# A seven-product form for two projections of a hybrid trunk layer, with low parts made by accumulating DMA

## The chip, the cores and the metric

The kernel runs on one core of a Trainium2 chip. The metric is the time of one execution on the device, in microseconds (us). In the views, PE is TensorE, PEld its weight load, DVE VectorE, ACT ScalarE, POOL GpSimd and SP SyncE.

## The reference

One layer with D = 1024 and 1024 positions, in f32, batch 1. Cut to what matters:

```python
h = rms_norm(x, norm_g) * (1 + scale) + shift           # scale, shift, gate from c
(sq, sk, sv, sz, dq, dk_, dv_, dz, db, da,
 lq, lk, lv, lz, lr, mg) = split(h @ w_in)              # one input projection
y_sb  = stick_breaking_attention(q, k, v) * silu(sz)    # 4 heads x 128  -> 512 wide
y_gdn = rms_norm(gated_delta_rule(...), gdn_onorm) * silu(dz)   # 512 wide
y_gla = rms_norm(gla_chunked(...), gla_onorm) * silu(lz)        # 4 heads x 256 -> 1024 wide
g_sb, g_gdn, g_gla = split(sigmoid(mg + merge_b), 3)    # three gates, D wide each
merged = g_sb*(y_sb @ proj_sb) + g_gdn*(y_gdn @ proj_gdn) + g_gla*(y_gla @ proj_gla)
return x + gate * (merged @ w_out)
```

The GLA projection and the output projection are products of 1024 x 1024 by 1024 x 1024; proj_sb and proj_gdn have 512 rows.

## The kernel before

Everything is kept transposed: 128 channels on the partitions, 1024 positions (two halves of 512, HALF) along the free dimension. Each f32 operand is split into a high part (a cast to a shorter form) and a low part (source minus high part), and a product takes three passes: high x high, high x low, low x high. `split` is a cast on ScalarE and a subtraction on VectorE (lines 151 and 152), or with a scale lines 154 and 155. `load_w` brings a weight of 128 columns in halves of 512 rows (256 KB, tile "raw") and splits each. `mm` (L95) issues every matmul; `run_cm` makes one group: two halves, each 3 x kt matmuls of 128x512 (kt is 8, or 4 for 512 rows) into one PSUM bank of the pool "acc", which has two banks, and then `evac` reads the bank.

TensorE's order is written out by hand (`emit`, `dense`): the mixers' steps are tasks with due times, and dense groups of the input projection fill the time between them. The other engines' orders are made by a scheduler. 18 of the 24 gate groups run early as fillers (`early_gate`) and keep their result in DRAM (`g_dram`); the mixers' results y go to DRAM too (`y_dram`: 0 to 3 SB, 4 to 7 GDN, 8 to 15 GLA).

After the last attention block comes the final stage, `final_groups`: GLA's first 512 rows for 8 column blocks d ("part", ScalarE copies the bank), then gates and GLA's other rows ("rest"), GDN ("add"), SB ("last"), and 8 groups of the output projection (`out_group`), whose operands are the split of the merged rows. There are 1440 matmuls of 128x512 in it: 6 gate groups x 48, 384 for GLA, 192 for GDN, 192 for SB, 384 for the output. `load_y` brings y in 512 KB pieces and splits them. The norm weights gla_onorm and gdn_onorm are multiplied into the weights proj_gla and proj_gdn when these are split, 128 rows at a time.

Of the kernel before, what the change touches and what calls it, by code (L numbers as in the profile page):

```python
# [19 lines left out]
P = 128  # L20
D = 1024
# [8 lines left out]
EARLY = [(g, d) for g in (1, 0, 2) for d in range(2, KT)]  # L30
# [22 lines left out]
def kernel(ctx: ExitStack, tc: tile.TileContext, xT: bass.AP, c: bass.AP,  # L53
# [6 lines left out]
    wp = ctx.enter_context(tc.tile_pool(name="wp", bufs=3))  # L60
# [96 lines left out]

    def raw_tile():
        return wp.tile([P, 4, P], F32, tag="raw", name="raw")

    def load_half(hi, lo, src, k0, scales=None):
        raw = raw_tile()
        nc.sync.dma_start(out=raw, in_=src[k0 * P:(k0 + 4) * P, :].rearrange("(k p) n -> p k n", p=P))
        if scales is None:
            split(hi, lo, raw)
        else:
            for k in range(4):
                split(hi[:, k, :], lo[:, k, :], raw[:, k, :], scales[k])
# [18 lines left out]
    def run_cm(w, evac, rhs=None, kt=KT):  # L187
        r_hi, r_lo = rhs or (h_hi, h_lo)
        late = getattr(evac, "late", None)
        for hf in range(2):  # L190
# [11 lines left out]
            evac(hf, sl, ps)  # L202
            yield

    def run_tm(w, evac):
        whi, wlo = w
        late = getattr(evac, "late", None)
        for t2 in range(CH // 2):
            ps = bank(pa, "acc", HALF)
            for j in range(2):  # L210
                ts = slice((2 * t2 + j) * P, (2 * t2 + j + 1) * P)
                n = 0
                for k in range(KT):
                    for r, b in ((h_hi, whi), (h_hi, wlo), (h_lo, whi)):
                        mm(ps[:, j * 256:(j + 1) * 256], r[k][:, ts], b[:, k, :], 109,
# [9 lines left out]
    # a dense group: (load, run); loads are issued one group ahead  # L225
# [103 lines left out]
    # the first head's four column groups advance together as h arrives  # L329
# [4 lines left out]
    for k in range(KT):  # L334
# [5 lines left out]
        w = wp.tile([P, 2, 4, P], F32R, tag="w", name="w")  # L340
# [387 lines left out]
    def gdn_scan(st, q):  # L728
# [49 lines left out]
        nc.vector.tensor_mul(out=y, in0=ps.rearrange("p c t -> p (c t)"), in1=st["z"][:, sl])  # L778
# [190 lines left out]
    def gla_scan(st, q):  # L969
# [37 lines left out]
        for o, t0, since in outs:  # L1007
# [8 lines left out]
            for e_ in range(2):  # L1016
                y = mid("w6", 256)
                nc.vector.tensor_mul(out=y, in0=ps[:, e_].rearrange("p i t -> p (i t)"),
                                     in1=st["z"][e_][:, t0:t0 + 256])
                nc.sync.dma_start(out=y_dram[8 + 2 * h + e_][:, t0:t0 + 256], in_=y)  # L1020

# [133 lines left out]
    merged = []  # L1155
    gate_t = {}
    ys = {}

    def gate_group(gi, d):
        def evac():  # L1160
            gate_t[gi, d] = mid("v0"), mid("v1")

            def f(hf, sl, ps):
                nc.scalar.activation(out=gate_t[gi, d][hf], in_=ps, func=AF.Sigmoid,
                                     bias=C("merge_b", gi * 8 + d))
            return f
        return cm_in(O_MG + gi * D + d * P, evac)

    def early_gate(gi, d):
# [13 lines left out]
        return cm_in(O_MG + gi * D + d * P, evac)  # L1183

    def fetch_gate(gi, d):
        def run(_):
            gate_t[gi, d] = mid("v0"), mid("v1")
            for hf in range(2):
                nc.sync.dma_start(out=gate_t[gi, d][hf],
                                  in_=g_dram[gi, d][:, hf * HALF:(hf + 1) * HALF])  # L1190
            return
            yield
        return (lambda: None), run

    def load_y(yi):
        hi, lo = [], []
        for k in range(4):
            yr = big("u3")
            nc.sync.dma_start(out=yr, in_=y_dram[yi + k])
            a, b = big(f"u{4 + k}", 1024, F32R), big(f"u{4 + k}", 1024, F32R)  # L1200
            split(a, b, yr)
            hi.append(a)
            lo.append(b)
        return hi, lo

    def proj_group(gi, proj, row0, yi, d, scales, mode):
        def evac(hf, sl, ps):
            if mode == "part":
                if hf == 0:
                    merged.append(big(("u0", "u1", "u2", "u8")[d // 2]))  # L1210
                nc.scalar.copy(out=merged[d][:, sl], in_=ps)
                return
# [171 lines left out]
```

## Time and profile before

| what | value |
|---|---|
| median of 3 runs | 1523.69 us (1520.3 to 1524.83) |
| span of the profiled execution | 1522.0 us |
| TensorE busy | 1463.0 us, 96% |
| VectorE busy | 861.8 us, 57% |
| ScalarE busy | 676.8 us, 44% |
| GpSimd busy | 175.8 us, 12% |
| TensorE in the final stage, 1181.5 to 1518.1 us | 336.56 of 336.60 us |
| mean granted clock | 0.987 |

The profiled execution's time is its span, 1522.0 us; no other time of it is given. Busy shares are over the whole span. The granted clock is a share of full speed.

### The profile page before, as it was taken

To read this page: it belongs to the slowest core of one execution; us is meant where nothing else is said; L and a number is where in the kernel's file an instruction comes from. 1 tells how busy PE (TensorE), PEld (TensorE's weight loads), DVE (VectorE), ACT (ScalarE), POOL (GpSimd) and SP (SyncE) were. 2 spreads that over 40 slices of the span, in tenths; PEclk is the share of its full clock that TensorE was granted. 3 is DMA by queue.
4 is the path that set the end of the run, shared out by engine and by line. 5 is a ranking of instruction groups with operands and counts; after the bars stand their busy time and mean duration, and the time that the engine had idled before them with its cause. 6 is when DMAs were issued, how large, how long until landed. Compare 5 with 4: busy or idle time off the path is not lost.

```text
span 1522.0 us, 26560 instructions
## 1 busy us (share of the span) xinstructions
PE 1463.0 (96%) x10564; PEld 1227.5 (81%) x10564; DVE 861.8 (57%) x1855; ACT 676.8 (44%) x1473; POOL 175.8 (12%) x306
## 2 busy tenths in 40 slices
PE   4898999999999999999999999999999999999998
PEld 1677787777778887978888999889988888888887
DVE  5978736557653666667666525563555226474621
ACT  4255845462652846556475524342444442322200
POOL 4231222223330000000000100000000000000000
PEclk8899999999999999999999999999999999999999
DMA  6644322131231211212121212111122334353342
GB/s 211 189 119 120 99 87 74 44 88 47 79 93 50 56 43 53 53 32 60 50 67 38 69 49 63 49 36 42 43 69 85 110 104 138 115 149 111 120 143 76
DMA packets 162470, 126.48 MB, mean 83 GB/s; under 512 B 23429, under 2 KB 139269, under 8 KB 162346
## 3 DMA queue, kind: packets, MB, share of 16 engines
q1 hardware_dynamic: 162202, 124.47, 27.9%
q8 instruction: 83, 1.36, 0.4%
q14 instruction: 41, 0.34, 0.1%
q10 hardware_dynamic: 144, 0.31, 0.1%
HBM read 99.80 MB, written 24.95 MB: 82 GB/s over the span
## 4 chain that ended last, share of the span: by engine, by line
PE 81%; DVE 9%; ACT 4%; POOL 2%; issue 2%; DMA 2%; SPq 0%; POOLq 0%; DVEq 0%; ACTq 0%
PE acc L95 66%; PE lv L95 6%; PE mx L95 6%; PE tr L122 3%; DVE u L299 1%; DVE w L152 1%; POOL c L284 1%; DVE u L386 1%; POOL u L453 1%; DVE w L570 1%; DVE w L572 1%; DVE u L1110 1%; DMA u<-in_adaT 1%; POOL w L596 0%; DMA w<-xd 0%
## 5 line engine op out<-in xcount | busy, mean ns | idle before, releaser
L95 PE MATMUL acc<-h_hi,w 128*128 128x512 f32 x1856 | 658.1, 409 | 12.4 <-ACT h_hi L151 5.7
L95 PEld LDWEIGHTS acc<-h_hi,w 128*128 128x128 f32 x1856 | 352.5, 190 | 84.5 <-ACT h_hi L151 6.1
L95 PE MATMUL acc<-h_lo,w 128*128 128x512 f32 x928 | 365.9, 394 | 8.1 <-DVE h_lo L358 7.7
L95 PEld LDWEIGHTS acc<-h_lo,w 128*128 128x128 f32 x928 | 176.9, 191 | 36.9 <-DVE h_lo L358 8.9
L95 PE MATMUL acc<-whi,h_hi 128*128 128x256 f32 x640 | 186.8, 292 | 0.0
L95 PE MATMUL acc<-whi,h_lo 128*128 128x256 f32 x640 | 180.7, 282 | 0.0
L95 PE MATMUL acc<-wlo,h_hi 128*128 128x256 f32 x640 | 180.7, 282 | 0.0
L95 PE MATMUL acc<-u,w 128*128 128x512 f32 x768 | 176.5, 391 | 0.0
L95 PEld LDWEIGHTS acc<-u,w 128*128 128x128 f32 x768 | 144.2, 188 | 31.6
L151 ACT CAST w<-raw 128x512 fp32r<-128x512 f32 x143 | 84.2, 619 | 121.8 <-PE acc L95 90.4
L152 DVE TENSOR_TENSOR w<-raw,w 128x512 fp32r<-128x512 f32 x143 | 98.5, 701 | 50.7 <-ACT w L151 49.9
L95 PEld LDWEIGHTS acc<-whi,h_hi 128*128 128x128 f32 x640 | 122.3, 191 | 1.4 <-issue 0.7
L95 PEld LDWEIGHTS acc<-wlo,h_hi 128*128 128x128 f32 x640 | 122.4, 191 | 0.1
L95 PEld LDWEIGHTS acc<-whi,h_lo 128*128 128x128 f32 x640 | 122.1, 191 | 0.0
L284 POOL TENSOR_TENSOR c<-c,mhalf 128x4 f32<-128x4 f32 (+1 forms) x56 | 54.7, 976 | 578.8 <-DVE c L282 577.4
L95 PE MATMUL acc<-m_hi,w 128*128 128x512 f32 x256 | 79.0, 389 | 0.0
L1110 DVE TENSOR_TENSOR_SCAN u<-u,zero_c 128x128 f32<-128x128 f32 (+7 forms) x32 | 43.4, 1356 | 36.1 <-ACT u L1108 36.1
L155 DVE SCALAR_TENSOR_TENSOR w<-raw,col,w 128x128 fp32r<-128x128 f32 x96 | 29.5, 349 | 55.3 <-ACT w L154 55.3
L95 PEld LDWEIGHTS mx<-r,u 128*128 128x128 f32 x288 | 44.1, 190 | 18.0 <-DVE r L751 4.9
L95 PEld LDWEIGHTS acc<-m_hi,w 128*128 128x128 f32 x256 | 48.0, 188 | 10.0
L95 PE MATMUL mx<-r,u 128*128 128x128 f32 x288 | 48.5, 281 | 6.3 <-POOL u L720 2.7
L95 PE MATMUL lv<-u,u 128*32 128x32 f32 (+5 forms) x528 | 49.2, 252 | 4.1 <-DVE u L653 4.1
(254 smaller groups left out, 2177.6 us busy)
## 6 DMA issues: line engine op xcount, KB each, us to landing
raw<-in_w_in SPq DMA_DIRECT2D x160, 256.0 KB, 3.0
u<-in_adaT SPq DMA_DIRECT2D x24, 512.0 KB, 3.5
g_dram<-v SPq DMA_DIRECT2D x36, 256.0 KB, 2.1
v<-g_dram SPq DMA_DIRECT2D x36, 256.0 KB, 2.6
u<-in_xT SPq DMA_DIRECT2D x16, 512.0 KB, 5.6
u<-y_dram SPq DMA_DIRECT2D x16, 512.0 KB, 3.8
v<-gam_d SPq DMA_DIRECT2D x16, 256.0 KB, 3.5
y_dram<-v SPq DMA_DIRECT2D x16, 256.0 KB, 2.0
```

Source lines behind the costliest of these rows:

```text
L95: return nc.tensor.matmul(out, lhsT=lhsT, rhs=rhs, **kw)
L122: nc.tensor.transpose(out=out, in_=in_, identity=ident[:k, :k])
L151: nc.scalar.copy(out=hi, in_=raw)
L152: nc.vector.tensor_sub(out=lo, in0=raw, in1=hi.bitcast(F32))
L155: nc.vector.scalar_tensor_tensor(out=lo, in0=raw, scalar=scale, in1=hi.bitcast(F32), op0=ALU.mult, op1=ALU.subtract)
L284: nc.gpsimd.tensor_tensor(out=out, in0=out, in1=mhalf[:, 0:n], op=ALU.pow)
L299: nc.vector.tensor_tensor_reduce(out=junk, in0=aw, in1=c_row, scale=1.0, scalar=0.0, op0=ALU.mult, op1=ALU.add, accum_out=mod[:, j:j + 1])
L386: nc.vector.scalar_tensor_tensor(out=t, in0=r[:, tap:tap + T], scalar=C("conv", j + tap), in1=t, op0=ALU.mult, op1=ALU.add)
L453: nc.gpsimd.tensor_scalar(out=gt[0][DA, sl], in0=raw[DA, :], scalar1=C("dt_bias")[DA, :], scalar2=None, op0=ALU.add)
L570: nc.vector.tensor_tensor(out=t3, in0=L3[:, w:16, j:w].broadcast_to([32, n, w]), in1=Xl3[:, j:w, 0:w].broadcast_to([32, n, w]), op=ALU.mult)
L572: nc.vector.tensor_sub(out=Xl3[:, w:16, 0:w], in0=Xl3[:, w:16, 0:w], in1=t3)
L1110: nc.vector.tensor_tensor_scan(om[:, 0:n][:, ::-1], om[:, 0:n][:, ::-1], zero_c.broadcast_to([P, n]), 1.0, ALU.mult, ALU.add)
```

## The change

**Seven products in place of eight.** The GLA and the output projection are taken as 2 x 2 blocks of 512: output columns d and d + 4 (d = p), the two halves of the positions, and the two halves of the 1024 rows. `strassen` makes a pair (p, p + 4) of output blocks from seven products of a combination of weight blocks (`PRODUCTS`) with a combination of operand blocks (`UNITS`: b11, t1, t2, b22, t3, b21, t4; t1 to t4 are differences). Each is 12 matmuls (4 row blocks x 3 passes), 84 for a pair, four pairs for a projection. Two PSUM banks accumulate: X takes units 0, 2, 4, 6 and W units 1, 3, 5; `read(i)` reads the bank after each unit.

**Operands of GLA.** The differences of y are formed during attention (tasks T.y0 to T.y3, `differences`: 4 loads, 4 subtractions and 4 stores each) and kept in DRAM; in the final stage each of 28 operands is loaded (256 KB), cast on ScalarE and subtracted on VectorE (`load_unit`).

**Operands of the output.** `out_operands(p)` is called after SB's group d = p + 4; its seven pieces form differences of the merged blocks and split them by `split_dma`: ScalarE writes the high part, then its negative into the low part, and GpSimd issues a DMA that adds the source to it. The weights of GDN, SB and the output use it as well, 72 in all.

**The rest.** All gates go through g_dram; six gate groups still run at the start of the final stage. The onorm weights are multiplied into y when it is made. The pool "raw" has 8 buffers where it had 3, the weight tiles are halved (6 for 3), the small weights are split in two halves, the order of the early gates is another, and the program has 4096 bytes for GpSimd's DMA descriptors. SB's and GDN's columns come in the order 0, 4, 1, 5, 2, 6, 3, 7.

```diff
+    def split_dma(hi, lo, raw):
+        nc.scalar.copy(out=hi, in_=raw)
+        nc.scalar.activation(out=lo, in_=hi.bitcast(F32), func=AF.Copy, scale=-1.0)
+        nc.gpsimd.dma_start(out=lo, in_=raw, accum_op=ALU.add)
...
+    def strassen(src1, src2, rhs, prepare, read, by_dma=False):
...
+        def run(loaded):
+            a, ws, context = loaded
+            ahead.pop(0)
+            while len(ws) < 3:
+                ws.append(part(a, len(ws)))
+            X, W = bank(pa, "acc", HALF), bank(pa, "acc", HALF)
+            for i, unit in enumerate(UNITS):
+                if i + 3 < 7:
+                    ws.append(part(a, i + 3))
+                else:
+                    early_part()
+                ps = X if i in (0, 2, 4, 6) else W
+                first, last = i in (0, 1, 5), i in (3, 5, 6)
+                n = 0
+                for p in range(4):
+                    for v, r in ((0, 0), (0, 1), (1, 0)):
+                        mm(ps, ws[i][:, v, p, :], rhs[p][unit][r], 216,
+                           start=(first and n == 0), stop=(last and n == 11),
+                           skip_group_check=True)
+                        n += 1
+                    if p == 1:
+                        yield
+                read(i, ps, context)
+                yield
...
+    def load_unit(tag, src):
+        hi, lo = new_unit(tag)
+        raw = lo.bitcast(F32)
+        nc.sync.dma_start(out=raw, in_=src)
+        nc.scalar.copy(out=hi, in_=raw)
+        nc.vector.tensor_sub(out=lo, in0=raw, in1=hi.bitcast(F32))
+        return hi, lo
...
+    def differences(n, p, get):
+        def sub(out, a, b, t):
+            nc.vector.tensor_sub(out=out, in0=a, in1=b)
+            nc.sync.dma_start(out=t_dram[n, p][t], in_=out)
...
+        def read(i, ps, xr):
...
+                nc.vector.scalar_tensor_tensor(out=x[:, ts], in0=ps[:, ts],
+                                               scalar=mod[:, 16 + d:17 + d], in1=x[:, ts],
+                                               op0=ALU.mult, op1=ALU.add)
...
     def final_groups():
...
+        gs = [gate(*e) for e in EARLY[sum(FILL):]]
+        gs[0] = after(lambda: gla_operands(FIRST_UNITS), gs[0])
+        gs += [after(lambda: gla_operands(("t3", "b21", "t4")), gla_pair(0))]
+        gs += [gla_pair(p) for p in range(1, 4)]
+        order = [d for p in range(4) for d in (p, p + 4)]
+        gs += [proj_group(1, proj_gdn, 4, d) for d in order]
+        gs += [proj_group(0, proj_sb, 0, d) for d in order]
+        gs += [out_pair(p) for p in range(4)]
+        return [(g, ["S.m3"]) for g in gs]
...
+    for p in range(4):
+        tasks.append((f"T.y{p}", lambda p=p: y_differences(p), ["L.s3.1", f"D.S{min(p, 2)}"], 0))
```

**First place: TensorE where one GLA column block or pair ends and the next begins.** In the kernel before, TensorE's list in the GLA part of the final stage reads so (acc_N is one use of a bank; u4 to u7 are y's parts, w a weight):

```order
L95 MATMUL acc_12864<-u6_12814,w_12789 128x512
L95 MATMUL acc_12864<-u6_12815,w_12789 128x512
L95 MATMUL acc_12864<-u6_12814,w_12789 128x512
L95 MATMUL acc_12864<-u7_12820,w_12789 128x512
L95 MATMUL acc_12864<-u7_12821,w_12789 128x512
L95 MATMUL acc_12864<-u7_12820,w_12789 128x512
L95 MATMUL acc_12879<-u4_12802,w_12789 128x512 [waits Activation_49]
L95 MATMUL acc_12879<-u4_12803,w_12789 128x512
L95 MATMUL acc_12879<-u4_12802,w_12789 128x512
```

Each new acc takes the other of the two banks. After the change, from the end of pair 0 to the start of pair 1 (acc_13491 is X of pair 0, acc_13492 its W; acc_13635 and acc_13636 are X and W of pair 1):

```order
L95 MATMUL acc_13492<-unit_13471,w_13539 128x512 x3
L95 MATMUL acc_13491<-unit_13475,w_13556 128x512 [waits DVE_49]
L95 MATMUL acc_13491<-unit_13475,w_13556 128x512 x2
L95 MATMUL acc_13491<-unit_13479,w_13556 128x512 x3
L95 MATMUL acc_13491<-unit_13483,w_13556 128x512 x3
L95 MATMUL acc_13491<-unit_13487,w_13556 128x512 x3
L95 MATMUL acc_13635<-u7_12962,w_13573 128x512 [waits DVE_49]
L95 MATMUL acc_13635<-u7_12962,w_13573 128x512 x2
L95 MATMUL acc_13635<-u7_12966,w_13573 128x512 x3
L95 MATMUL acc_13635<-u8_12970,w_13573 128x512 x3
L95 MATMUL acc_13635<-u8_12974,w_13573 128x512 x3
L95 MATMUL acc_13636<-u0_12978,w_13592 128x512 [waits DVE_49,Activation_49]
```

Unit 6 of a pair and unit 0 of the next stand next to each other on the same bank, and the first matmul of unit 0 waits for VectorE.

**Second place: GpSimd and TensorE from SB to the output.** GpSimd's list in the kernel before ends in the attention:

```order
L284 TENSOR_TENSOR c3_11952<-c3_11952,mhalf_116 128x4 [waits DVE_49,Pool_49]
L1053 MEMSET c2_12155 128x4 [waits Activation_49,Pool_49]
L284 TENSOR_TENSOR c3_12058<-c3_12058,mhalf_116 128x4 [waits DVE_49,Pool_49]
L284 TENSOR_TENSOR c3_12162<-c3_12162,mhalf_116 128x4 [waits DVE_49,Pool_49]
L1380 UNCONDITIONAL_BRANCH
L1380 ISA [waits barrier_Pool_Activation_PE_DVE_SP_gather]
```

After the change, these DMAs stand there around the end of SB (v2 to v4 hold differences, unit, u3 and u7 operands' parts or merged rows, w and raw a weight):

```order
L162 DMA unit_14890<-unit_13947 128x512 [waits DMASW7_49,DVE_49,Activation_49]
L162 DMA w_14945<-raw_14862 128x512 [waits DMASW0_49,PE_49,Activation_49]
L162 DMA w_14963<-raw_14808 128x512 [waits DMASW1_49,PE_49,Activation_49]
L162 DMA unit_14896<-v2_14894 128x512 [waits DMASW2_49,DVE_49,Activation_49]
L162 DMA w_14980<-raw_14812 128x512 [waits DMASW3_49,DMAHW1_49,PE_49,Activation_49]
L162 DMA u7_14886<-v4_14884 128x512 [waits DMASW4_49,DVE_49,Activation_49]
L162 DMA unit_14902<-v3_14900 128x512 [waits DMASW5_49,DVE_49,Activation_49]
L162 DMA unit_14906<-u7_13948 128x512 [waits DMASW6_49,Activation_49]
L162 DMA u3_14912<-v2_14910 128x512 [waits DMASW7_49,DVE_49,Activation_49]
L162 DMA u3_14916<-u7_13948 128x512 [waits DMASW0_49,Activation_49]
L162 DMA w_14997<-raw_14810 128x512 [waits DMASW1_49,DMAHW6_49,PE_49,Activation_49]
L162 DMA u4_14922<-v4_14920 128x512 [waits DMASW2_49,DVE_49,Activation_49]
```

And TensorE's list in unit 2 (t2) of the first output pair (acc_14942 is X), where DMASW names a DMA of GpSimd:

```order
L95 MATMUL acc_14942<-unit_14558,w_14864 128x512 [waits DVE_49]
L95 MATMUL acc_14942<-unit_14558,w_14864 128x512
L95 MATMUL acc_14942<-unit_14558,w_14864 128x512 [waits DMASW0_49]
L95 MATMUL acc_14942<-u5_14678,w_14864 128x512
L95 MATMUL acc_14942<-u5_14678,w_14864 128x512 [waits DMASW4_49]
L95 MATMUL acc_14942<-u5_14678,w_14864 128x512
L95 MATMUL acc_14942<-u1_14798,w_14864 128x512
L95 MATMUL acc_14942<-u1_14798,w_14864 128x512 [waits DMASW3_49]
L95 MATMUL acc_14942<-u1_14798,w_14864 128x512
L95 MATMUL acc_14942<-unit_14902,w_14864 128x512 [waits Activation_49]
L95 MATMUL acc_14942<-unit_14902,w_14864 128x512 [waits DMASW5_49]
L95 MATMUL acc_14942<-unit_14902,w_14864 128x512
```

GpSimd goes from nothing to a row of DMAs, each behind ScalarE, and TensorE's low-part passes wait for them one by one.

**Third place: VectorE late in the attention.** Before (mx, tr: PSUM; u5, u6: rows of attention weights, L1112 their difference after the scan of L1110):

```order
L155 SCALAR_TENSOR_TENSOR u3_10300<-tr_10642,col_86,u2_10299 128x256 [waits Activation_49]
L1110 SCALAR_TENSOR_TENSOR u6_10652<-u6_10652,zero_c_118 128x1024 [waits Activation_49]
L1112 TENSOR_TENSOR u5_10651<-u5_10651,u6_10652 128x1023 [waits DVE_49,Activation_49]
L282 TENSOR_SCALAR c3_10687<-c2_10680 128x4 [waits Activation_49]
L152 TENSOR_TENSOR wlo_10699<-raw_10700,whi_10698 128x4x128 [waits DMAHW3_49,PE_49,Activation_49]
L1061 TENSOR_TENSOR v1_10690<-acc_10593,c3_10687 128x512 [waits Pool_49]
L152 TENSOR_TENSOR wlo_10699<-raw_10704,whi_10698 128x4x128 [waits DMAHW6_49,Activation_49]
L152 TENSOR_TENSOR wlo_10699<-raw_10708,whi_10698 128x4x128 [waits DMAHW7_49,Activation_49]
L1133 COPY v2_10729<-tr_10724 128x512 [waits PE_49]
```

After the change, in the attention of the second head (L1137 is the scan, L1139 the difference, L1301 a difference of y):

```order
L1137 SCALAR_TENSOR_TENSOR u6_11428<-u6_11428,zero_c_118 128x896 [waits Activation_49]
L1139 TENSOR_TENSOR u5_11427<-u5_11427,u6_11428 128x895 [waits DVE_49,Activation_49]
L1301 TENSOR_TENSOR raw_11782<-raw_11788,raw_11782 128x512 [waits DMAHW3_49]
L1301 TENSOR_TENSOR raw_11788<-raw_11788,raw_11784 128x512 [waits DMAHW4_49,DVE_49]
L1160 COPY v2_11468<-tr_11463 128x512 [waits PE_49]
L1103 TENSOR_TENSOR u4_11334<-u4_11334,acc_11403 128x512 [waits Activation_49]
L1160 COPY v2_11473<-mx_11470 128x256 [waits PE_49]
L152 TENSOR_TENSOR w_11480<-raw_11481,w_11480 128x512 [waits DMAHW1_49,Activation_49]
L1301 TENSOR_TENSOR raw_11794<-raw_11794,raw_11788 128x512 [waits DMAHW6_49,DMAHW1_49,DVE_49]
L1137 SCALAR_TENSOR_TENSOR u6_11501<-u6_11501,zero_c_118 128x1024 [waits Activation_49]
L1301 TENSOR_TENSOR raw_11800<-raw_11798,raw_11800 128x512 [waits DMAHW5_49,DMAHW7_49,DMAHW0_49,DVE_49]
L1139 TENSOR_TENSOR u5_11500<-u5_11500,u6_11501 128x1023 [waits DVE_49,Activation_49]
```

VectorE's list has the subtractions of y between the steps of attention, each behind loads on SP's queue (DMAHW).

## Rows read from the trace of the kernel before

**Rows 1.** The page: busy time by engine, granted clock, chain by engine.
```profile
PE 1463.0 (96%) x10564; PEld 1227.5 (81%) x10564; DVE 861.8 (57%) x1855; ACT 676.8 (44%) x1473; POOL 175.8 (12%) x306
...
PEclk8899999999999999999999999999999999999999
...
PE 81%; DVE 9%; ACT 4%; POOL 2%; issue 2%; DMA 2%; SPq 0%; POOLq 0%; DVEq 0%; ACTq 0%
```

**Rows 2.** Busy time by stretch: us, engines' busy (instructions), clock, DMA share, GB/s.
```profile
0.00:200.00 200.00, 162.07 (x790) 124.10 (x791) 153.89 (x324) 107.83 (x185) 60.35 (x79) 0.91 0.49 145
880.00:1181.50 301.50, 297.60 (x2051) 271.23 (x2050) 149.81 (x227) 109.51 (x300) 13.52 (x22) 1.00 0.19 56
1181.50:1518.10 336.60, 336.56 (x1476) 276.77 (x1475) 149.30 (x258) 88.86 (x177) 0.00 (x0) 1.00 0.39 119
1387.50:1431.10 43.60, 43.60 (x192) 35.74 (x192) 34.18 (x48) 13.54 (x19) 0.00 (x0) 1.00 0.43 133
1431.10:1518.10 87.00, 86.96 (x384) 71.64 (x382) 21.07 (x30) 7.86 (x13) 0.00 (x0) 1.00 0.34 109
```

**Rows 3.** The chain that ended last, its end: start us, us, what.
```profile
1181.49 336.58 PE acc L95 x1476
...
1518.10 0.48 DVE v L1252
```

**Rows 4.** Timeline, end of the output stage: start us, us, engine, line, operation.
```profile
1507.22 0.75 DVE L1252 SCALAR_TENSOR_TENSOR v<-acc,mod,u 128x512 f32<-128x512 f32 x1 [4.69 <-PE acc L95]
1512.66 0.75 DVE L1252 SCALAR_TENSOR_TENSOR v<-acc,mod,u 128x512 f32<-128x512 f32 x1 [4.69 <-PE acc L95]
...
1517.67 0.39 PE L95 MATMUL acc<-m_hi,w 128*128 128x512 f32 x1
...
1518.10 0.88 DVE L1252 SCALAR_TENSOR_TENSOR v<-acc,mod,u 128x256 f32<-128x256 f32 x2 [4.69 <-PE acc L95]
```

**Rows 5.** Timeline of TensorE and VectorE near 1020 us, around a wait.
```profile
1020.30 0.63 PE L122 MATMUL tr<-cst,u 128*128 128x128 f32 x4 [0.65 <-DVE u L155]
1020.80 0.47 PE L95 MATMUL acc<-h_hi,w 128*128 128x512 f32 x1
...
1019.67 0.48 DVE L155 SCALAR_TENSOR_TENSOR u<-tr,col,u 128x256 fp32r<-128x256 f32 x1
1020.16 0.69 DVE L1076 TENSOR_TENSOR u<-u,acc 128x512 f32<-128x512 f32 x1
```

**Rows 6.** Timeline of ScalarE: a dependent pair, and two casts in a row.
```profile
1184.38 0.69 ACT L1175 ACTIVATE v<-acc,col 128x512 f32<-128x512 f32 x1
1185.10 0.63 ACT L1180 ACTIVATE v<-v 128x512 f32<-128x512 f32 x1
...
1223.19 1.15 ACT L151 CAST w<-raw 128x512 fp32r<-128x512 f32 x2
```

**Rows 7.** DMA issues of the final stage: count, KB each, median us to landing.
```profile
v<-g_dram SPq DMA_DIRECT2D x36, 256.0 KB, 2.6
u<-y_dram SPq DMA_DIRECT2D x12, 512.0 KB, 4.3
...
g_dram<-v SPq DMA_DIRECT2D x2, 256.0 KB, 2.1
```

**Rows 8.** DMA view of the first 130 us: GB/s in 40 slices.
```profile
GB/s 95 326 373 420 417 309 183 234 18 0 91 0 42 153 178 168 242 229 226 172 241 205 234 276 104 136 45 282 169 38 0 33 101 155 178 107 135 0 5 43
```

**Rows 9.** Timeline, early: VectorE beside GpSimd's work and after; GpSimd's slow step.
```profile
29.00 2.83 DVE L152 TENSOR_TENSOR w<-raw,w 128x512 fp32r<-128x512 f32 x1
...
46.12 0.68 DVE L152 TENSOR_TENSOR w<-raw,w 128x512 fp32r<-128x512 f32 x1
...
100.84 8.96 POOL L453 TENSOR_SCALAR u<-v,col 4x512 f32<-4x512 f32 x1
...
110.71 1.56 POOL L453 TENSOR_SCALAR u<-v,col 4x512 f32<-4x512 f32 x1
```

**Rows 10.** Attention: VectorE's timeline, and TensorE's waits from 880 to 1181.5 us.
```profile
1051.97 0.69 DVE L1149 TENSOR_TENSOR v<-mx,u 128x512 f32<-128x512 f32 x1 [5.25 <-PE mx L95]
...
PE tr L122 <- DVE v L1133: 2.1, 2, 1.3
```

More of the change, by code (lines that the diff above doesn't have):

```diff
@@ L29 @@
 EPS = 1e-6
[L30 removed]
+EARLY = [(g, d) for g in (1, 0, 2) for d in range(KT)]
 FILL = (5, 1, 4, 0, 0, 0, 2, 1, 1, 4)
@@ L202, in run_cm @@
             evac(hf, sl, ps)
+            if hf == 0 and soon is not None:
+                for _ in range(3):
+                    soon()
             yield
@@ L1152, in sb_mix, with early_part, gate @@
             yield 1200
[L1155 to L1169, printed above, removed]
+    ahead = []
+    def early_part():
+        if ahead:
+            ahead[0]()
+    def gate(gi, d):
         def evac():
@@ L1182, in evac @@
             return f
[L1183 to L1193, printed above, removed]
+        o = O_MG + gi * D + d * P
+        return (lambda: load_w(w_in[:, o:o + P])), (lambda w: run_cm(w, evac(), soon=early_part))
@@ L1195, in load_y @@
+    ys = {}
+    Y_TAGS = {4: ("u8", "u0", "u1", "u2"), 0: ("u3", "u4", "u6", "h")}
     def load_y(yi):
         hi, lo = [], []
[L1197 to L1201, printed above, removed]
+        for k, tag in enumerate(Y_TAGS[yi]):
+            a, b = unit_tile(tag), unit_tile(tag)
+            raw = b.bitcast(F32)
+            nc.sync.dma_start(out=raw, in_=y_dram[yi + k])
+            nc.scalar.copy(out=a, in_=raw)
+            nc.vector.tensor_sub(out=b, in0=raw, in1=a.bitcast(F32))
@@ new lines, in evac @@
+            def evac(hf, sl, ps):
+                t = mid("v4")
+                nc.vector.tensor_mul(out=t, in0=g[hf], in1=ps)
+                nc.vector.tensor_add(out=merged[d][:, sl], in0=merged[d][:, sl], in1=t)
+                for piece in pieces[:2]:
+                    piece()
+                del pieces[:2]
+            yield from run_cm(w, evac, ys[yi], 4, soon=early_part)
+            if gi == 0 and d >= 4:
+                out_operands(d - 4)
+            if gi == 0 and d == KT - 1:
+                for piece in pieces:
+                    piece()
@@ new lines, in after, with with_fn @@
+    def after(fn, group):
+        load, run = group
+        def with_fn(w):
+            fn()
+            yield from run(w)
+        return load, with_fn
+    def final_groups():
+        gs = [gate(*e) for e in EARLY[sum(FILL):]]
[7 more added lines that the diff above has]
+        return [(g, ["S.m3"]) for g in gs]
```

268 lines of the change are left out of this document (185 added, 83 removed).

## The prediction

> **What bounds the kernel now.** I read the head of the page first: TensorE is busy for 96% of a span of 1522.0 us, VectorE for 57%, ScalarE for 44%, GpSimd for 12%, and the granted clock is at nine tenths or more after the first two slices [rows 1]. The median of the runs shown is 1523.7, 1.7 above that span; the sum below is made against the span, and 1.7 is added at the end. The table by stretch says where TensorE is not busy: about 38 us in the first 200, 4 between 880 and 1181 (attention), 0.04 in the final stage from 1181.5 to 1518.1 [rows 2]. The chain that ended last closes with 336.58 us of TensorE, 1476 matmuls with no wait between them, and then VectorE's last step of the output [rows 3]. So the final stage is pure matmul: each 128x512 matmul taken out there is worth one pitch, and each new wait there costs its full length. Out of it come 96 matmuls; the question is what waits go in.
>
> **What it removes.** GLA before: 8 columns x 2 halves x 24 matmuls = 384; after: 4 pairs x 7 products x 12 = 336. The output projection is the same, so 96 fewer in all. The pitch: two readers of the output stage that are 24 matmuls apart start 5.44 us apart [rows 4], 0.2267 each; the whole chain gives 336.58/1476 = 0.228. Gain 96 x 0.227 = **21.8 us** (21.8 to 21.9). The rest of TensorE's list is the same up to this stage.
>
> **Joints between pairs.** A pair uses bank X for units 0, 2, 4, 6 and W for 1, 3, 5. Unit 6 and the next pair's unit 0 are both on X, so TensorE must wait until unit 6 has been read (the first order piece). Nothing in before waits so: there the bank changed every 12 or 24 matmuls and the reader had a whole group's time. From rows: a matmul ends 0.39 after its start, where the next would start after 0.227, thus 0.16; the reader starts 0.04 after that end (1517.67 + 0.39 = 1518.06, then 1518.10) [rows 4]; it takes 0.75 for the output's form, 0.69 for a 512-wide product [rows 4, 5]; TensorE starts 0.15 after VectorE's end (1020.15 to 1020.30), and the first matmul after a wait takes 0.47 in place of 0.39 [rows 5]. That is 1.18 or 1.12. There are seven such places: GLA to GLA three times, GLA to GDN once, output to output three times: 4 x 1.12 + 3 x 1.18 = **8.0 us lost**. If the restart is hidden it is 0.95 each (6.6); if VectorE still has an older 0.69 step to finish at each GLA joint, 4 x 0.69 more (10.8).
>
> **Split by accumulating DMA.** For the 16 GDN and SB weights, the 28 output weights and the 28 output operands, ScalarE writes the high part and its negative, and GpSimd issues a DMA that adds the f32 source to it: 72 of them. VectorE loses its subtraction (0.69), ScalarE gains a step: two casts in a row take 1.15, a dependent pair of 512-wide steps starts its second 0.72 after the first [rows 6], so about 1.2 per split. ScalarE is under half used there and this alone is hidden. Before has no DMA issued by GpSimd, so its price is bounded: from below 2.1 us to landing (a 256 KB store) and 2.6 (the load of a gate), from above 4.3 (a 512 KB load, since the accumulation must also read what it adds to) [rows 7]. I take 4, as it reads twice. In engine time, the sixteen DMA engines moved 420 GB/s in their fullest slice [rows 8], so 256 KB takes 0.62 us of all of them, and 1.25 if the target is read as well.
>
> The Trainium skill, page "DMA: Bandwidth & Descriptors", section "Anatomy of one DMA — SWDGE (gpsimd) path", gives a fixed 2.0 us and then bytes at 436 GB/s for such a DMA, by which I estimate 2.6 us for 256 KB; no run here shows it yet. With 2.6 in place of 4 the next term would be 1.5 us smaller.
>
> **SB to output.** This is the tight place. The output's operands are made from merged blocks, which the SB groups finish one after another; the last, t2 of p = 3, waits for the very last SB group. After its last matmul: two VectorE steps (0.69 each) for the merge and one for t2, then ScalarE's queue with a cast and a negation per operand or weight (about three splits stand there, 1.2 each): the negative stands 5.5 us after the last SB matmul. Plus 4 for the DMA is 9.5. TensorE wants t2's low part at 2 x 2.72 + 10 x 0.227 = 7.7. Stall about 2. Next late after it: t3, t4 of p = 3, which share ScalarE and GpSimd and the small tiles v2 to v4, so each round trip of a DMA counts again. And 37 accumulations (28 operands, 9 weights) fall between 38.5 us before the end of SB and 18.8 after it, when the last is due: 57 us. At 1.25 they fill 46 us of that, and in the SB stage the engines were already busy at 0.43 [rows 2]. So I take **4 us**, with 0.5 (DMA of 2.6, uncrowded) and 12 (46 + 0.34 x 57 = 65 us of work in 57, on top of the 2 and of slow tiles) as ends.
>
> **The other edits.** Gates to GLA: the 28 operands (7 units x 4 row blocks, for all pairs) are loaded from DRAM, 256 KB each with a cast and a subtraction, behind six gate groups of 48 x 0.227 = 10.9 us each; only the last nine wait for tiles of h, first due 11 us into the pair: 0.5. GLA to GDN: y of GDN is loaded (512 KB, 4.3), cast and subtracted under units 3 to 6 of the last pair (10.9 us): 1, for order on ScalarE. Differences of y during attention: 16 subtractions of 0.69 us, 16 loads and 16 stores; VectorE has gaps there (5.25 us ahead of one step), and the largest of TensorE's waits for it is 2.1 us in all [rows 10], so **0.5** (0 to 4: if a chunk of subtractions stands ahead of a scan that TensorE waits for, see the third order piece). The onorm scale moves into the product that makes y (0.75 for 0.69), and the 96 small scalings of weights (4 for each of 24 halves) go: off the path. Deeper raw buffers reshuffle VectorE's first 100 us, where 38 us of TensorE wait: 0, with 5 to either side.
>
> **Sum.** -21.8 + 8.0 + 4 + 0.5 + 1 + 0.5 = -7.8: span 1514.2, median about **1516**. A difference under 0.3% (4.6 us) can't be told from none here, so faster means below 1519.1.
>
> **Rivals.**
> - *Accumulations late, gain eaten.* The stall at SB to output is 7 to 16: 1519 to 1528, the same. For it: the count of engine time above. Against: only the last few operands are due at once; others have 20 us and more.
> - *Other side: accumulations go one by one through GpSimd's queue*, each keeping the next for c us. Then the 37th is done at 37c - 38.5, due at 18.8: stall 37c - 57. With the gain of 11.8 that is left before this term, it is slower than before from c = 1.86, and by 0.3% from c = 2.0. At c = 2.1, the time of a store to its landing, the stall is 21 and the time 1533; at 2.6 it is 39 and 1551. For it: nothing shows whether such a DMA's issue waits for the one before. Against: loads on SP's queue overlap (0.62 us per 256 KB at 420 GB/s is far under the 2.6 to landing).
> - *GpSimd held by VectorE.* A TENSOR_SCALAR of GpSimd took 8.96 once and 1.56 the next time, and VectorE's subtraction 2.83 beside GpSimd's work against 0.68 without [rows 9]. If each issue waits out one VectorE step of 0.69 on top of 0.9, c = 1.6, the stall is 2 to 3 there, in place of the 2 above, but every chain of v tiles is longer too: 6 in all, 1518. The Trainium skill, page "SBUF — State Buffer", section "SBUF: two separate sides", warns that VectorE's copies in a two-port mode keep GpSimd from writing descriptors. The rows agree that the two hold each other up; VectorE's steps in the SB stage are two-input ones, and no run here yet shows a DMA's issue beside them.
> - *Cheaper than thought.* Joints of 0.95, a stall of 0.5, start-up 3 better: 1508.
> - *No effect of what it says*: excluded for the 96 matmuls, which the order shows gone.
>
> **Chances.** Forecast with its own range 1511 to 1519: 0.42, with GpSimd held (1516 to 1519) 0.06; cheaper, 1504 to 1511: 0.14; late accumulations, 1519 to 1528: 0.18; one by one, 1528 to 1551: 0.20. Faster 0.42 + 0.06 + 0.14 = 0.62, same 0.18, slower 0.20. The range 1507 to 1532 leaves out some 0.05 below and 0.14 above.
>
> **What would show it.** From the end of attention on there should be 1380 matmuls where 1476 stood; at the seven joints a wait for VectorE of about 0.9 to 1 us by the list of waits; between SB and output a few waits for a DMA, in sum 2 to 6 us; GpSimd's DMAs should land in about 4 us and overlap. Wrong would be: GpSimd's DMAs in single file with 2 us or more each, ScalarE as the one waited for at the output, or the first 200 us changed by over 5 us.

## The result and the profile after

The change makes the kernel slower: 1539.1 us in the median of four runs (1534.8 to 1542.1) against 1523.7 for three runs of the kernel before, a ratio of 1.0107 (1.008 to 1.0133). A fourth run of the kernel before, at 5583 us, was disturbed and is left out. The forecast was 1516 in a range of 1507 to 1532. The profiled execution took 1534.8 us with a span of 1533.0, that is 11.0 more than the span of the kernel before (1522.0).

The page of the kernel after (busy time by engine; the DMA engines' share in 40 slices; the queue of GpSimd's DMAs; their landing):

```profile
PE 1451.9 (95%) x10468; PEld 1211.6 (79%) x10468; DVE 890.3 (58%) x1850; ACT 737.4 (48%) x1547; POOL 233.0 (15%) x379
...
DMA  6743322131332111121212231324225243879995
...
q0 software_dynamic: 10368, 18.88, 7.1%
...
w<-raw POOLq DMA_DIRECT2D x44, 256.0 KB, 5.3
```
TensorE's busy time fell by 11.1 us, not by 21.8, and the DMA engines stand at 7 to 9 tenths in five of the last six slices, where they stood at 2 to 5 tenths before. GpSimd's 72 DMAs took 7.1% of sixteen engines: 0.071 x 1533.0 / 72 = 1.51 us of all of them each. The 44 for weights land after 5.3 us in the median.

The table by stretch answers to [rows 2]:

```profile
880.00:1181.50 301.50, 297.93 (x2051) 271.47 (x2052) 167.02 (x250) 115.63 (x308) 13.52 (x22) 1.00 0.31 93
1181.50:1533.00 351.50, 324.64 (x1377) 261.07 (x1375) 153.86 (x225) 142.36 (x240) 63.41 (x72) 0.98 0.70 181
1340.00:1350.00 10.00, 7.99 (x28) 6.40 (x29) 5.68 (x8) 2.05 (x4) 0.86 (x1) 0.83 0.97 265
1420.00:1430.00 10.00, 8.45 (x27) 6.36 (x27) 4.05 (x7) 4.00 (x8) 4.40 (x5) 0.75 1.11 264
1460.00:1470.00 10.00, 6.47 (x22) 4.91 (x21) 2.01 (x3) 3.72 (x7) 2.66 (x3) 0.83 1.01 271
```
The attention is as before. The final stage has 324.64 us of matmul in place of 336.56, where 1380/1476 of that is 314.7, and waits. From 1181.5 to the last matmul's end (1529.14) it lasts 347.6 us, 11.0 more than before: -21.9 for the 96 matmuls, +23.0 for waits, +9.9 for matmuls that are slower. Some 2 us of these are the last matmul's end ahead of each of 12 waits, 0.16 each; the rest lies with the clock, which was 0.83, 0.75 and 0.83 in the ten-microsecond stretches around the ends of the three waits of 3.2 to 3.8 us. The waits of TensorE in the stage (us in total, times, longest):

```profile
PE acc L95 <- DVE v L1393: 6.1, 3, 3.2
PE acc L95 <- ACT u L160: 3.8, 1, 3.8
PE acc L95 <- DVE v L1448: 3.7, 2, 2.2
PE acc L95 <- ACT w L160: 3.5, 1, 3.5
PE acc L95 <- DMA unit<-v: 2.9, 2, 2.1
PE acc L95 <- DMA unit<-unit: 1.6, 1, 1.6
PE acc L95 <- ACT v L1356: 1.1, 1, 1.1
PE acc L95 <- DVE v L1361: 0.3, 1, 0.3
```
and where the three longest stand (the bracket is the idle time ahead):

```profile
1342.01 18.17 PE L95 MATMUL acc<-u,w 128*128 128x512 f32 x71 [3.20 <-DVE v L1393]
...
1419.60 4.18 PE L95 MATMUL acc<-u,w 128*128 128x512 f32 x9 [3.83 <-ACT u L160]
...
1465.00 2.08 PE L95 MATMUL acc<-unit,w 128*128 128x512 f32 x6 [3.52 <-ACT w L160]
```
By place: GLA to GDN 4.6 us, the SB stage 6.7, the first output pair 4.5, the second and third output pairs 7.2 (the wait at 1465.00 at the start of the second, 2.2 and 1.5 at unit 2 of either). For the most part TensorE is let go by VectorE and ScalarE; what these two stand for is one step further back. VectorE in the SB stage:

```profile
1418.17 0.69 DVE L1422 TENSOR_TENSOR v<-unit 128x512 f32<-128x512 f32 x1 [6.49 <-DMA unit<-v]
1418.78 0.68 DVE L1393 TENSOR_TENSOR v<-v,acc 128x512 f32<-128x512 f32 x1
```
It forms a difference (L1422) in a small tile that is still the source of an accumulating DMA, stands 6.49 us for it, and the reader of the PSUM bank (L1393) stands behind; its end at 1419.46 and TensorE's start at 1419.60 are 0.14 apart. At the start of the second output pair it is the same with a weight's tile. The chain of waits, and VectorE's row behind it:

```profile
1454.79 8.63 DMA w<-raw
...
1463.50 0.70 DVE raw L1239
...
1464.27 0.63 ACT w L160
...
1465.00 7.36 PE acc L95 x24
...
1464.11 1.40 DVE L1448 SCALAR_TENSOR_TENSOR v<-acc,mod,v 128x512 f32<-128x512 f32 x2
```
An accumulating DMA of the combination s2 takes 8.63 us; then VectorE may form s4 in the tile that was its source (L1239). ScalarE's cast of s4 and the next two bank readers stand behind it; the cast ends at 1464.90, the first reader at 1464.86, and TensorE starts at 1465.00. Whichever of the two let it go, the 3.52 above come from the held tile. VectorE's own waits for such DMAs from 1385 to 1500 us:

```profile
DVE raw L1239 <- DMA w<-raw: 12.0, 3, 6.8
DVE v L1422 <- DMA unit<-v: 6.5, 1, 6.5
...
DVE raw L1234 <- DMA w<-raw: 6.1, 1, 6.1
...
DVE raw L1237 <- DMA w<-raw: 1.8, 1, 1.8
```
The same hold stops SP's queue, which issues the loads in the order of its list: the next weight is to be loaded into a tile that is still such a source. Its waits for that in the same stretch:

```profile
SPq L175 <- DMA w<-raw: 32.3, 12, 7.6
```
The loads behind in the list go out late with it, those of operands that no accumulating DMA touches among them.

### The profile page after: what moved, and what is told of

Same layout as the page of the kernel before. It is cut to its first block, busy times and chain, and to the rows that moved or that the text cites. A ratio compares the mean times of both kernels' runs of the same rounds, so it can differ in the third digit from the quotient of the medians.

```text
span 1533.0 us, 26920 instructions
## 1 busy us (share of the span) xinstructions
PE 1451.9 (95%) x10468; PEld 1211.6 (79%) x10468; DVE 890.3 (58%) x1850; ACT 737.4 (48%) x1547; POOL 233.0 (15%) x379
## 3 DMA queue, kind: packets, MB, share of 16 engines
q0 software_dynamic: 10368, 18.88, 7.1%
## 4 chain that ended last, share of the span: by engine, by line
PE 70%; DVE 12%; DMA 8%; ACT 4%; issue 3%; POOL 2%; SPq 0%; DVEq 0%; POOLq 0%; ACTq 0%
PE acc L95 57%; PE lv L95 5%; PE mx L95 5%; PE tr L122 2%; DVE w L595 1%; DVE w L152 1%; DVE u L406 1%; DMA v<-g_dram 1%; DMA u<-in_adaT 1%; DVE u L319 1%; DMA w<-raw 1%; DVE w L593 1%; DMA u<-v 1%; POOL c L304 1%; DMA v<-gam_d 1%
## 5 line engine op out<-in xcount | busy, mean ns | idle before, releaser
L95 PE MATMUL acc<-w,h_hi 128*128 128x256 f32 x1280 | 238.8, 287 | 0.0
L152 DVE TENSOR_TENSOR w<-raw,w 128x512 fp32r<-128x512 f32 x187 | 129.4, 700 | 124.2 <-ACT w L151 121.8
L95 PEld LDWEIGHTS acc<-w,h_hi 128*128 128x128 f32 x1280 | 198.7, 191 | 1.5 <-issue 0.7
L151 ACT CAST w<-raw 128x512 fp32r<-128x512 f32 x187 | 113.7, 619 | 141.6 <-PE acc L95 122.0
L95 PE MATMUL acc<-w,h_lo 128*128 128x256 f32 x640 | 180.8, 282 | 0.0
L95 PEld LDWEIGHTS acc<-w,h_lo 128*128 128x128 f32 x640 | 122.2, 191 | 0.0
L95 PE MATMUL acc<-unit,w 128*128 128x512 f32 x312 | 83.0, 401 | 13.3 <-DVE v L1448 3.7
L162 POOL DMA_DIRECT2D w<-raw x44 | 39.2, 912 | 314.3 <-DVE unit L1364 197.6
L95 PEld LDWEIGHTS acc<-unit,w 128*128 128x128 f32 x312 | 59.1, 191 | 29.6 <-ACT w L161 4.5
L1194 ACT ACTIVATE v<-acc,col 128x512 f32<-128x512 f32 x48 | 32.9, 685 | 83.9 <-PE acc L95 83.3
L1137 DVE TENSOR_TENSOR_SCAN u<-u,zero_c 128x128 f32<-128x128 f32 (+7 forms) x32 | 43.4, 1357 | 35.1 <-ACT u L1135 35.1
L160 ACT CAST w<-raw 128x512 fp32r<-128x512 f32 x44 | 26.9, 616 | 74.5 <-PE acc L95 55.2
```

Source lines behind the costliest of these rows:

```text
L95: return nc.tensor.matmul(out, lhsT=lhsT, rhs=rhs, **kw)
L151: nc.scalar.copy(out=hi, in_=raw)
L152: nc.vector.tensor_sub(out=lo, in0=raw, in1=hi.bitcast(F32))
L160: nc.scalar.copy(out=hi, in_=raw)
L162: nc.gpsimd.dma_start(out=lo, in_=raw, accum_op=ALU.add)
L1137: nc.vector.tensor_tensor_scan(om[:, 0:n][:, ::-1], om[:, 0:n][:, ::-1], zero_c.broadcast_to([P, n]), 1.0, ALU.mult, ALU.add)
```

## The experiments

Times are medians in us; "before" ran on the same chip each time. What was expected was written ahead of each run.

| kernel | low parts by accumulating DMA | us | before | ratio (95%) |
|---|---|---|---|---|
| the change | 72 | 1539.1 | 1523.7 | 1.0107 (1.008 to 1.0133) |
| a_all_vector | 0 | 1514.7 | 1522.1 | 0.9958 (0.9941 to 0.9974) |
| b_operands_vector | 44 weights | 1527.6 | 1522.1 | 1.0039 (1.0024 to 1.0053) |
| c_weights_vector | 28 operands | 1516.7 | 1522.1 | 0.9967 (0.9957 to 0.9976) |
| d_plain_dma | 72, copying only | 1517.9 | 1522.1 | 0.9969 (0.9956 to 0.9981) |
| f_early_two_dma | 14 operands | 1516.4 | 1520.6 | 0.9970 (0.9956 to 0.9985) |
| g_early_three_dma | 21 operands | 1512.4 | 1520.6 | 0.9943 (0.9925 to 0.9962) |
| e_joint | 14 operands | 1514.2 | 1520.6 | 0.9958 (0.9944 to 0.9972) |
| h_before_weights_dma | 24, in the kernel before | 1528.2 | 1520.6 | 1.0050 (1.0034 to 1.0067) |
| l_blocks_dma | 10 merged blocks | 1505.6 | 1520.9 | 0.9903 (0.9885 to 0.9920) |
| m_blocks_sb_weights | 10 blocks, 8 weights | 1505.8 | 1520.9 | 0.9906 (0.9890 to 0.9923) |
| n_fixed_banks | 10 blocks | 1513.6 | 1520.9 | 0.9952 (0.9938 to 0.9966) |
| o_differences_dma | 10 differences | 1510.7 | 1520.5 | 0.9939 (0.9919 to 0.9959) |

**All on VectorE.** In `split_dma`:

```diff
-        nc.scalar.copy(out=hi, in_=raw)
-        nc.scalar.activation(out=lo, in_=hi.bitcast(F32), func=AF.Copy, scale=-1.0)
-        nc.gpsimd.dma_start(out=lo, in_=raw, accum_op=ALU.add)
+        split(hi, lo, raw)
```

> All 72 low parts are subtracted on VectorE again; the seven-product form and everything else stay. Theory 1 (the accumulating DMAs: 18.9 MB took 30.8% of the sixteen engines over 352 us, 1.5 us of all of them per DMA, and 5 to 9 us to landing; so the 23.0 us of waits and the 9.8 us of slowed matmuls behind them in the final stage all come from them, directly or through other loads made late): the span falls by 28 to 33 us, to 1500 to 1505, so 1502 to 1507 in time, about 20 faster than the kernel before. Theory 2 (the waits come from the seven-product order itself: in-place differences, buffers held, more loads): 1525 to 1540 as now. Theory 3 (VectorE becomes the bound in SB and output, with 50 us more work): a loss of waits for DMA but 10 us or more of waits for VectorE's subtraction, 1512 to 1525.

The 24 us between 1539.1 and 1514.7 (23 by the ratios) go with `split_dma`, that is the accumulating DMAs and ScalarE's second step; theory 2 falls. But the 1502 to 1507 of theory 1 were not reached, and theory 3 says why. Busy time up to SB and in it, and TensorE's two waits left:

```profile
1181.50:1390.00 208.50, 208.32 (x909) 170.25 (x908) 111.15 (x165) 70.78 (x115) 0.00 (x0) 1.00 0.49 150
1390.00:1430.00 40.00, 37.37 (x154) 29.62 (x152) 39.34 (x66) 17.52 (x32) 0.00 (x0) 0.96 0.38 114
```
```profile
1424.11 3.33 PE L95 MATMUL acc<-unit,w 128*128 128x512 f32 x8 [1.82 <-DVE unit L152]
...
1432.66 1.65 PE L95 MATMUL acc<-unit,w 128*128 128x512 f32 x3 [3.47 <-DVE v L1446]
```
Up to 1390 us TensorE has no gap to speak of (208.32 of 208.50), so the seven products of GLA bring no wait. Then VectorE is busy 39.34 of 40 us, and TensorE waits for it at the start of the output, 5.3 us, with 3.33 us for 8 matmuls behind a wait.

**Which of the 72.** Operands alone on VectorE (`split` in `out_operands`), and weights alone (`split` in `load_w` and `part`).

> Only the 28 output operands are subtracted on VectorE; the 44 weights keep the accumulating DMA. Theory 1: the waits at the end of SB (6.7 us) and in the first output pair (4.5) go, those of GLA to GDN (4.6) stay, those between output pairs (7.2) stay at least in part, because there a weight's DMA is what is waited for; 1518 to 1528. If the operands alone were the trouble: 1502 to 1510. If the weights alone were: no change, 1535 to 1541.

> Only the 44 weights are subtracted on VectorE; the 28 output operands keep the accumulating DMA. Theory 1: the waits of GLA to GDN (4.6 us) and between output pairs (7.2) go with the slow clock behind them, those at the end of SB and in the first output pair (11.2) shrink but do not vanish, since the engines' load in those 60 us falls from 37 DMAs to 28; 1508 to 1520. If the weights alone were the trouble: 1502 to 1508; if the operands alone: 1535 to 1541.

Both times as theory 1 had them. The weights are the worse part: with them on the DMA TensorE still waits for the output's bank readers (L1448) three times, 3.0, 3.2 and 3.5 us. From 1385 to 1500 us VectorE stands 15.8 us and SP's queue 24.2 us for DMAs of weights there; with the operands on the DMA it is 12.1 and 4.9, with all low parts on VectorE nothing.

**Copy in place of addition.**

```diff
-        nc.gpsimd.dma_start(out=lo, in_=raw, accum_op=ALU.add)
+        nc.gpsimd.dma_start(out=lo.bitcast(F32), in_=raw)
```

> GpSimd's 72 DMAs copy the source in place of adding it to the negative: the low part is left uncorrected (it is the source itself), the number of DMAs, their issue and their bytes as counted stay. If the cost is the read of the target that accumulation needs: the engines' time per DMA falls from 1.5 us to about 0.75, landing from 5 to 9 down to 3 to 4, and the time to 1508 to 1520. If it is that GpSimd issues them (0.87 us each, behind ScalarE) or any third stream of this size: engines' time and landing hardly fall and the time stays at 1530 to 1540.

This kernel leaves the addition out, so its low part is the source itself. The same two rows of its page:

```profile
q0 software_dynamic: 5760, 18.88, 3.3%
...
w<-raw POOLq DMA_DIRECT2D x44, 256.0 KB, 3.6
```
0.033 x 1517.7 / 72 = 0.70 us of all engines per DMA in place of 1.51, landing 3.6 in place of 5.3, packets 80 for each in place of 144, and 21 us off the time. ScalarE's second step and the 72 DMAs of GpSimd are still there, so these are not the 21 us; they are what the DMA does beyond copying. That the target is moved too fits the doubled engine time but is not seen in the bytes, which the page counts as 18.88 MB for both. Two things came along with the addition and were not separated from it: the target is of type fp32r in the one and f32 in the other, and GpSimd's issue fell from 912 to 552 ns in the mean of the 44 for weights (GpSimd is busy 63.41 of 351.5 us in the stage, so that is a small part). The hold is not gone with the copy: from 1385 to 1500 us VectorE still stands 18.9 us and SP's queue 23.3 for GpSimd's DMAs, where it was 27.6 and 41.8 in the change.

**Fewer of them.** Operands of p = 0 and 1, or 0 to 2, by DMA, the rest on VectorE:

```diff
-            split_dma(hi, lo, src)
+            (split_dma if p < 2 else split)(hi, lo, src)
```

> Output operands of p = 0 and 1 (14, wanted 20 us and more after they are made) keep the accumulating DMA; those of p = 2 and 3 and all weights are subtracted on VectorE. With everything on VectorE that engine was busy without a gap from about 1389 to 1437 us, and TensorE waited 5.5 us for it, with some 6 us of slow clock behind. Taking 14 x 0.6 = 8.4 us off that row: the waits fall to 0 to 2 us, the slow clock goes, 1502 to 1508. If not VectorE's load but the order of the last operands sets those waits: 1512 to 1516. If 14 DMAs suffice to crowd the engines: 1514 to 1520.

> The same with p = 0, 1 and 2 by DMA (21), only p = 3 on VectorE. Crowding theory: between the kernel with 14 and the one with all 28 by DMA (1517): 1506 to 1514. If VectorE's load is all that matters: as good as 14 or better, 1502 to 1506.

With 14 it is no better than with none or with all 28: the 1502 to 1508 expected were missed, and VectorE's load was not all. Its row in the SB stage shows what else:

```profile
1414.28 0.69 DVE L1422 TENSOR_TENSOR v<-unit 128x512 f32<-128x512 f32 x1 [5.72 <-DMA unit<-v]
1414.88 0.68 DVE L1393 TENSOR_TENSOR v<-v,acc 128x512 f32<-128x512 f32 x1
```
5.72 us at a difference whose tile a DMA still reads, the bank reader behind it, and TensorE 3.06 us without work. With 21 this wait stays (2.83), but VectorE has less to do at the output's start, where TensorE waits 1.2 us in place of 4.7; hence 1512.4. This made the theory of the held source: a merged block may be the source of such a DMA, since nothing writes it again, a difference in v2 to v4 may not.

```diff
+            (split_dma if name == "b11" or name[0] == "b" and p < 3 else split)(hi, lo, src)
```

> Only ten output operands that are plain merged blocks (b11 of all p, b22 and b21 of p = 0 to 2) keep the accumulating DMA; differences and weights are subtracted on VectorE. With 14 or 21 by DMA, VectorE stood up to 5.7 us at a difference whose small tile was still the source of a DMA in flight, and the bank readers stood behind it, so TensorE waited 3 us in the SB stage. Source-held theory: a merged block is never written again in that time, so no such wait is left; VectorE has 10 x 0.6 = 6 us less than with everything on it; the SB stage shows no wait, the one at the first output pair falls under 2 us, and the time is 1503 to 1509. If the wait there comes from VectorE's load alone, still 1509 to 1513; if any accumulating DMA in SB does harm: 1513 to 1518.

1505.6, and all of TensorE's waits in the final stage:

```profile
PE acc L95 <- DMA unit<-unit: 0.4, 1, 0.4
PE acc L95 <- DVE v L1448: 0.4, 1, 0.4
PE acc L95 <- DVE v L1393: 0.3, 1, 0.3
```
The contrast, ten differences in place of ten blocks:

> The contrast to the kernel with ten merged blocks by DMA: here ten differences keep it (t1 to t4 of p = 0 and 1, t1 and t3 of p = 2), and blocks and weights are subtracted on VectorE. Number of DMAs and VectorE's relief are the same; what differs is the source, a small tile that VectorE writes again for the next p. Source-held theory: VectorE stands for a DMA at a difference again (3 us or more in all), the bank readers behind it, TensorE waits 2 us or more in the SB stage with slow clock behind it, 1510 to 1517. If only the number of DMAs and VectorE's load count: 1503 to 1509, as with the blocks.

1510.7, 5.1 more, with VectorE again standing for GpSimd's DMAs around SB, where with ten blocks it stands for none:

```profile
DVE v L1393 <- DMA u<-v: 2.3, 1, 2.3
...
DVE v L1422 <- DMA unit<-v: 1.2, 1, 1.2
```
SP's queue stands 4.9 us for one more, again where none was with the blocks. TensorE waits 4.1 us in the final stage in place of 1.1. Which operands come late differs as well, but TensorE waits for a DMA 0.4 us at most in either. So the hold of the source is shown with the number of DMAs and VectorE's work unchanged; its size for ten is at the lower end of what was expected. How the 24 us of all 72 divide between the hold and the engines' time was not measured apart.

**Eight more whose source is not rewritten.**

> As the kernel with ten blocks by DMA, and the eight SB weights by accumulating DMA too, whose source tiles VectorE does not write. VectorE's load theory: another 8 x 0.6 = 5 us less, so 1500 to 1507. Crowd theory (18 DMAs of 1.5 us on top of the loads, and raw tiles held longer, which delays the loads of the output weights): 1508 to 1516.

No change: eight more whose source VectorE does not write neither help nor harm. Some relief and some crowd may cancel here; that was not separated.

**The banks.** W is taken before X, on the kernel with 14 operands by DMA; and, on the kernel with ten blocks, one pair of PSUM tiles for all pairs of a projection:

```diff
-            X, W = bank(pa, "acc", HALF), bank(pa, "acc", HALF)
+            if not banks:
+                banks.extend(bank(pa, "acc", HALF) for _ in range(2))
+            X, W = banks
```

> The kernel with 14 operands by DMA, but in each pair bank W is taken before bank X. The prediction held that unit 6 and the next pair's unit 0 share a bank and paid 8.0 us for seven such joints; the trace after shows no such wait, as the first bank taken is the one that was read earlier. If so, here unit 0 does land on unit 6's bank, and the time rises by 6.6 to 10.8 us over the kernel with 14 operands by DMA. If banks simply alternate whatever is taken first, nothing changes.

> As the kernel with ten blocks by DMA, but the four pairs of a projection use the same two PSUM tiles, so unit 6 of a pair and unit 0 of the next are on one bank for certain, as the prediction assumed for all. Taking bank W first changed nothing. If the prediction's price is right where the bank is shared (1.12 and 1.18 us a joint), six joints add 6.9 us (5.7 to 8.5), with waits of 0.8 to 1 us for VectorE at each; if TensorE gets over a shared bank more cheaply, under 3 us.

In the kernel after, around the first joint:

```profile
1267.73 5.63 PE L95 MATMUL acc<-unit,w 128*128 128x512 f32 x24
1273.20 3.16 PE L95 MATMUL acc<-u,w 128*128 128x512 f32 x13
...
1271.12 0.68 DVE L1361 TENSOR_TENSOR v<-v,acc 128x512 f32<-128x512 f32 x1
...
1273.53 0.68 DVE L1364 TENSOR_TENSOR unit<-v,acc 128x512 f32<-128x512 f32 x1
```
Unit 0 of the next pair starts at 1273.20, ahead of unit 6's reader (1273.53), so it is on another bank, the one whose reader (1271.12) is done. At none of the seven joints does TensorE wait for unit 6's reader: the wait at the start of the second output pair ends at 1465.00, and that reader, the second of the two above, at 1465.51. The order in which the two are taken does not matter (1514.2 against 1516.4, within their spread; a rise of 6.6 to 10.8 was expected); why, was not found. With fixed banks:

```profile
1273.74 5.40 PE L95 MATMUL acc<-unit,w 128*128 128x512 f32 x23
1280.04 2.34 PE L95 MATMUL acc<-u,w 128*128 128x512 f32 x9 [0.90 <-DVE unit L1367]
...
1279.30 0.68 DVE L1367 TENSOR_TENSOR unit<-v,acc 128x512 f32<-128x512 f32 x1
```
Here TensorE does wait for unit 6's reader, 0.78 to 1.28 us at each of the six places (5.8 in all, to which the 0.16 and 0.08 at the two ends come), and the time is 8.0 us more (1513.55 against 1505.58), 1.3 for each. The price of a joint was about right; in the change there is none to pay.

**The DMA in the kernel before.**

> The kernel before, with the 8 SB weights and the 16 halves of the output weights split by accumulating DMA (24 DMAs, one per 3.6 us on average, made one group of 11 us ahead). If such a DMA is harmful in itself (GpSimd's issue, ScalarE's second step, its landing): slower by 3 us or more. If only the crowd of 37 in 57 us is: within 0.3% of the kernel before, 1518 to 1527, with landings of 3 to 5 us.

Slower by 0.5%, 7.6 us, so such a DMA harms without the crowd too. TensorE's two waits are at the output's start, and the chain behind them starts with the same hold, at the tile that the next weight is loaded into:

```profile
1421.53 5.35 DMA w<-raw
...
1426.95 4.21 DMA raw<-in_w_out
...
1431.18 0.62 ACT w L159
...
1437.07 0.50 PE L95 MATMUL acc<-m_hi,w 128*128 128x512 f32 x1 [1.74 <-ACT m_hi L151]
...
1438.33 0.50 PE L95 MATMUL acc<-m_lo,w 128*128 128x512 f32 x1 [0.76 <-DVE m_lo L152]
```
SP's queue has to wait for the accumulating DMA before it can load, ScalarE stands 4.84 us for that load, and the cast of the merged rows comes behind. That is 2.5 us of the 7.6 between the medians; the profiled span is 2.8 over that of the kernel before. Where the rest is was not settled.

## Why the prediction was wrong

The terms of its sum, and what the profiled execution has in their places (us):

| term | forecast | measured |
|---|---|---|
| 96 matmuls fewer | -21.8 | -21.9 |
| seven joints | +8.0 | 0 |
| SB to output: SB stage and first pair | +4 (0.5 to 12) | +11.2 |
| GLA to GDN | +1 | +4.6 |
| second and third output pairs | none | +7.2 |
| slower matmuls around the waits | none | +9.9 |
| gates to GLA, differences of y | +1.0 | 0 |
| sum | -7.8 | +11.0 |

**The gain** is there for the most part: GLA's part runs without a gap, and the kernel with ten blocks by DMA, which keeps every product of the change, has 18.4 us less of TensorE's busy time (1444.6), 1.1 us of waits in the final stage, and is 15.3 us under the kernel before.

**The joints** were priced about right and put where there are none: two uses of a bank that follow each other in the order's names were taken for one bank. The order shows that the first matmul waits for VectorE, not for which of its steps. That no joint was to be paid was luck: with it the forecast would have missed by some 8 us more.

**The split by accumulating DMA** is the step that failed. The prediction held ScalarE's second step to be hidden (the copying kernel keeps it and is within 3.2 us of the one without it), and sought the cost of the DMAs themselves in one place, SB to output, at 4 us. They cost 24 us against VectorE's subtraction in their place, and 33 against the kernel with ten blocks (31 by the ratios), at four places. Three things were missing. First, the size: 1.51 us of all engines was estimated at 1.25, and the landing, put at 4, was 5.3 in the median for the weights and up to 8.7 for operands. By the prediction's own count 37 x 1.51 + 0.34 x 57 = 75 us of transfers in 57 would have given a stall of 18 where 11.2 us of waits stood, so that count alone does not give the wait. Second, the hold: what writes the source of such a DMA again waits until it has landed, 5 to 9 us later. VectorE stood 26.4 us for that (the rows above), with the readers of PSUM behind it, and SP's queue 32.3. The prediction named the small tiles only as one more round trip for the last operands, not as a wait at the head of VectorE's list or of SP's. Third, other loads: at GLA to GDN a load of y landed after 7.04 us and the gate ahead of TensorE's 3.20 after 7.15, where the kernel with no such DMA has 5.27 and 3.69 and TensorE waits 0.2. And a long wait was priced at its length; with the clock around its end, it cost about a third more.

**The rivals.** *Late accumulations* was the right one: its stall of 7 to 16 holds the 11.2 measured at its place, and it missed the two other places and the slower matmuls. *One by one* is false in its mechanism: a second issue starts 0.9 us after the first, and each is in flight for some 5 us (5.3 in the median); that its range holds 1539 is luck. *GpSimd held by VectorE* is false: an issue took 0.9 us (912 ns in the mean of the 44 for weights), the figure that the prediction used without a row for it, with VectorE busy half the time and no step of VectorE added to it. So the warning of the Trainium skill (page "SBUF — State Buffer", "SBUF: two separate sides") does not reach these two-input steps here. The Trainium skill's figure for a DMA of GpSimd (page "DMA: Bandwidth & Descriptors", "Anatomy of one DMA — SWDGE (gpsimd) path"), 2.6 us for 256 KB by my estimate, is below both measured ones, 3.6 for the copy and 5.3 for the addition, in busy queues; the measurement decides.

**Attention and start-up** were put at 0.5 and 0: TensorE's busy time is 297.93 for 297.60 us in the one and the final stage begins within 1 us of where it did.

## What to carry to other kernels

An operation moved from an engine to an accumulating DMA has three prices: engine time on all queues (here 1.5 us per 256 KB, twice that of a copy), the landing, and the hold of its source until then. Look for who writes the source next, a step of an engine or a load, and what stands behind it in the same list. Here the change was 1% faster than the kernel before with ten such DMAs from tiles that nobody writes again, 0.6% with ten from tiles that are rewritten, 0.4% with none, and 1% slower with all 72. A wait for an engine in the program's order does not say which step is waited for, so whether two neighbours share a bank has to be seen in a trace.

## What was not expected of the hardware

An accumulating DMA of 256 KB took 1.51 us of the sixteen engines, 144 packets and 912 ns of GpSimd to issue, a plain one by the same queue 0.70, 80 and 552. Around the ends of TensorE's waits of 3.2 to 3.8 us the granted clock was 0.75 to 0.83 in ten microseconds, that is at the lower of its two levels (1.2 of 2.4 GHz) for part of them; the eight waits of 0.75 to 1.28 us in the kernel with fixed banks left it at 0.99 or more in the table by stretch. The length of a wait does not decide it alone: behind 1.82 us in the kernel with all low parts on VectorE 8 matmuls took 3.33 us (clock 0.59 from 1424 to 1428), while behind 2.91 us with the 28 operands by DMA 9 took 2.32 (clock 1.00).
